# Local attention of a hybrid decoder: the last head pair's projection, two of its three chunks placed behind the scores of two units

## The chip, the cores and the metric

The kernel runs on one core of one Trainium2 chip. Its time is the device time of one execution in microseconds (us). Before the change the median of 3 runs is 2169.54 us (2169.17 to 2170.61). A difference of 0.2%, 4.3 us, is about what a measurement of this kernel can tell from no change.

## What is computed

A two-layer decoder reads 1024 prompt tokens and 8 decode tokens (one new token for each of 8 sequences). Layer 0 is gated linear attention with attention to a memory, layer 1 is sliding-window attention with attention to a memory; each has an MLP. The change lies in the mixer of layer 1. There the normalised tokens are projected to 12 query heads of width 64 and to 4 memory queries. Each query block of 128 tokens looks at the 128 tokens before each of its tokens; 12 query heads share 4 key/value heads, a learned sink joins the softmax, and a bias depends on the distance:

```python
q, qm = split_cols(h @ w_in_b[bl], IN_B_SIZES)
...
def sink_attention(q, k, v, bias, valid, sinks):
    s = jnp.einsum('...qhgd,...khd->...hgqk', q, k).astype(jnp.float32) * (SWA_HEAD_DIM ** -0.5) + bias
    s = jnp.where(valid, s, -jnp.inf)
    sink = sinks.astype(jnp.float32).reshape(SWA_KV_HEADS, SWA_GROUP)[:, :, None, None]
    m = jnp.maximum(jnp.max(s, axis=-1, keepdims=True), sink)
    p = jnp.exp(s - m)
    p = (p / (jnp.sum(p, axis=-1, keepdims=True) + jnp.exp(sink - m))).astype(v.dtype)
    return jnp.einsum('...hgqk,...khd->...qhgd', p, v)
...
mix = jnp.concatenate([o_main, o_mem], axis=-1) @ w_out[l]
```

The 8 decode tokens do the same against cached keys and values (127 positions and their own), and attend to cached memories of 256 positions.

## The kernel before

Activations lie transposed: 128 partitions by 8 slabs of the model width by tokens, in three chunks of 384, 384 and 264 tokens (`CH`; the third holds the last 256 prompt tokens and the 8 decode tokens). Each chunk is kept as a high part and a low part (tiles `xh0`, `xl0` to `xh2`, `xl2`), weights likewise (`wh`, `wl`), and `proj` (L255) multiplies each of the 8 slabs three times: 24 matmuls in one PSUM bank for one block of 128 output features and one chunk.

`in_b(m)` (L1905) is the query projection of head pair m: it loads and splits the pair's weight, then runs `proj` for the three chunks. Each result is scaled into `q` by one DVE operation (L1912), which frees its PSUM bank. The banks come from a pool of two (`mmps`, names `mm`), taken in turn.

`swa(t, i2)` (L1914), called a unit here and written (t, i2), is local attention of head pair t for the two query blocks 2·i2 and 2·i2+1. There are 6 times 4 units. A unit's steps are:

- scores on PE (L1937) into the double bank `sA`, of which there is one; or, for t of 4 and 5 with i2 of 0 and 2, into two banks `mm`;
- four reductions on DVE (L1945), which read the scores, add the bias and take the maximum; then small operations (L1949, L1951);
- four exponentials on ACT (L1959) with sums, two small operations on DVE (L1961, L1963), and one multiplication of the 128 by 768 tile `z` on DVE (L1965);
- six transposes on PE (L1971, L1974) into the double bank `sT`, of which there is one, and its copy to `pt` on ACT (L1976);
- 32 value products on PE (L1982) into banks `sf` and `sx`, and two copies to `q` on ACT (L2005).

`swa_dec()` is local and memory attention of the decode tokens. It is a generator: each of the eight units with t of 4 and 5 first runs its next piece. Its buffers are cut from the tiles of X, which no one needs once the projections are done: `Arena(["xl2", "xh2", "xh1", "xl1", "xh0"])`. Of the eight memory key tiles (`in_mem_kT`, 256 KB each) two fall in `xl2`, four in `xh2` and the last two in `xh1`; the cached keys (`in_swa_kT`) fill the rest of `xh1`, the cached values (`in_swa_v`) and a zeroed query tile lie in `xl1`, and bias and results in `xh0`. All these names print as `ar`. Its loads are issued by POOL, and a load into a tile of X waits for the last matmul that reads that tile. Its steps on the engines are: copies of the memory query (L528, DVE), memory scores (L544, PE, with L554 to L560 on DVE behind), eight copies of the local query (L2036, DVE), local scores (L2050, PE), its softmax (L2054 to L2064), two transposes with four copies (L2068, L564, L2071, L567), and the value products (L2079, and L544 again).

Before the change the loop over t is: for t up to 4 `in_b(t)`, at t of 3 also `in_b(5)` directly behind it, then the four units of t. `in_b(4)` thus stands between the units of t=3 and those of t=4 in the program's text.

The order on each engine is not that of the text. A scheduler goes through the instructions, knows their data dependencies, their buffers and the priorities that the text gives, and writes a fixed order for each engine; engines then work strictly through their lists and wait on semaphores for each other. `add_manual_dep(a, b, NOSYNC)` adds to that planning that a comes behind b on the engine; it adds no wait.

After the last unit the output projection `out_proj` follows: `make_o1` splits `q` into a high and a low part (casts L158 on ACT, L159 on DVE), and 8 feature blocks by 24 matmuls run for each chunk.

## Time and profile before

| | |
|---|---|
| median of 3 runs | 2169.54 us (2169.17 to 2170.61) |
| the profiled execution | 2170.4 us, its span 2168.5 us |
| PE busy | 2130.6 us (98% of the span) |
| DVE, ACT, POOL busy | 1519.3 us (70%), 1092.4 us (50%), 117.1 us (5%) |
| mean granted TensorE clock | 0.997 |

All places below are given in us from the start of the span. PE is TensorE's matmuls, PEld its weight loads, DVE VectorE, ACT ScalarE, POOL GpSimd; a number with L is a line of the kernel. In a row of the timeline stand start, duration, engine, line, operation, output and input tile, shapes and count; a bracket gives the idle time just ahead of it and what ended it. Matmuls overlap, so a row's duration is longer than the step from one matmul to the next. In a row of windows stand the stretch, its length, the busy time of PE, PEld, DVE, ACT and POOL with the number of instructions, the granted TensorE clock (1.00 is full), the DMA engines' share and GB/s. Local attention takes from 1268 to 1417 us; the last eight units begin at about 1367.

### The profile page before, as it was taken

The numbers are of one execution on the slowest core, as the hardware profiler recorded it, in microseconds if no ns is written. First come the engines' busy times: TensorE is split into PE (matmuls) and PEld (weight loads), VectorE is DVE, ScalarE is ACT, GpSimd is POOL, SyncE is SP. The second block draws the span as 40 slices with busy tenths as digits, with TensorE's granted clock in tenths as the row PEclk, the third lists the DMA queues.
The fourth block names the chain that finished last, engine by engine and source line by source line (L and its number), as shares of the span: only waits on it lengthen the run. The fifth ranks groups of instructions, "written<-read, shape, count | busy, mean of one in ns | idle before, by whom it ended". The sixth has DMA issues, their size and how long they took to land.

```text
span 2168.5 us, 41912 instructions
## 1 busy us (share of the span) xinstructions
PE 2130.6 (98%) x16934; PEld 2037.4 (94%) x16934; DVE 1519.3 (70%) x2838; ACT 1092.4 (50%) x2196; POOL 117.1 (5%) x178
## 2 busy tenths in 40 slices
PE   8999999999999999999999999899999999999998
PEld 6879999899999999999999878699999999999998
DVE  7646648768887776856787355647987777764767
ACT  6354536557545444333654354646755545433453
POOL 0012000000000000134100000200000000000011
PEclk9999999999999999999999999999999999999999
DMA  5412026543654459666444201524374345935244
GB/s 170 145 68 76 24 66 171 158 131 126 197 162 129 141 163 324 223 229 233 148 133 151 63 11 32 166 65 157 116 221 142 133 162 208 325 117 172 96 135 148
DMA packets 141670, 316.39 MB, mean 146 GB/s; under 512 B 15833, under 2 KB 57873, under 8 KB 141121
## 3 DMA queue, kind: packets, MB, share of 16 engines
q1 hardware_dynamic: 123552, 268.32, 38.7%
q0 software_dynamic: 8880, 32.54, 4.5%
q10 hardware_dynamic: 9040, 12.82, 1.6%
q8 instruction: 134, 2.20, 0.4%
q14 instruction: 64, 0.52, 0.1%
HBM read 220.97 MB, written 93.74 MB: 145 GB/s over the span
## 4 chain that ended last, share of the span: by engine, by line
PE 89%; DVE 4%; ACT 3%; DMA 3%; issue 1%; SPq 0%; ACTq 0%; DVEq 0%
PE mm L263 17%; PE mx L263 9%; PE mx L851 6%; PE mx L853 6%; PE mx L852 6%; PE mx L1089 5%; PE mx L1090 5%; PE mx L1091 5%; PE mm L851 3%; PE mm L853 3%; PE mm L852 3%; PE mm L1089 2%; PE mm L1090 2%; PE mm L1091 2%; PE sx L1089 1%; PE sx L1091 1%
## 5 line engine op out<-in xcount | busy, mean ns | idle before, releaser
L158 ACT CAST wh<-ws 128x512 fp32r<-128x512 f32 (+1 forms) x258 | 185.8, 722 | 312.4 <-PE mx L852 99.4
L851 PE MATMUL mx<-xf,wh 128*128 128x258 f32 x1048 | 296.9, 283 | 0.0
L853 PE MATMUL mx<-xf,wl 128*128 128x258 f32 x1048 | 295.7, 282 | 0.0
L852 PE MATMUL mx<-xf,wh 128*128 128x258 f32 x1048 | 295.5, 282 | 0.0
L263 PE MATMUL mm<-xh,wh 128*128 128x384 f32 (+1 forms) x864 | 282.0, 326 | 1.5 <-DVE qx L1874 0.6
L263 PE MATMUL mm<-xh,wl 128*128 128x384 f32 (+1 forms) x864 | 278.4, 322 | 0.0
L263 PE MATMUL mm<-xl,wh 128*128 128x384 f32 (+1 forms) x864 | 277.9, 322 | 0.0
L159 DVE TENSOR_TENSOR wl<-ws,wh 128x512 fp32r<-128x512 f32 (+1 forms) x258 | 210.4, 817 | 53.7 <-ACT wh L158 48.0
L158 ACT CAST wh<-wr 128x1024 fp32r<-128x1024 f32 x102 | 106.9, 1048 | 276.8 <-PE sx L1090 261.3
L1089 PE MATMUL mx<-sa,wh 128*128 128x258 f32 x840 | 237.4, 283 | 0.0
L1090 PE MATMUL mx<-sa,wh 128*128 128x258 f32 x840 | 235.9, 281 | 0.0
L1091 PE MATMUL mx<-sa,wl 128*128 128x258 f32 x840 | 235.9, 281 | 0.0
L159 DVE TENSOR_TENSOR wl<-wr,wh 128x1024 fp32r<-128x1024 f32 x102 | 126.5, 1240 | 137.1 <-ACT wh L158 136.9
L852 PEld LDWEIGHTS mx<-xf,wh 128*128 128x128 f32 x1048 | 198.0, 189 | 0.4
L851 PEld LDWEIGHTS mx<-xf,wh 128*128 128x128 f32 x1048 | 197.6, 189 | 0.4
L853 PEld LDWEIGHTS mx<-xf,wl 128*128 128x128 f32 x1048 | 197.8, 189 | 0.0
L263 PEld LDWEIGHTS mm<-xh,wh 128*128 128x128 f32 x864 | 162.7, 188 | 11.2 <-issue 6.3
L263 PEld LDWEIGHTS mm<-xl,wh 128*128 128x128 f32 x864 | 162.7, 188 | 6.8 <-issue 5.3
L263 PEld LDWEIGHTS mm<-xh,wl 128*128 128x128 f32 x864 | 162.4, 188 | 6.9 <-issue 4.9
L1089 PEld LDWEIGHTS mx<-sa,wh 128*128 128x128 f32 x840 | 159.0, 189 | 0.1
L1090 PEld LDWEIGHTS mx<-sa,wh 128*128 128x128 f32 x840 | 158.7, 189 | 0.1
L1091 PEld LDWEIGHTS mx<-sa,wl 128*128 128x128 f32 x840 | 158.3, 188 | 0.0
(578 smaller groups left out, 5783.2 us busy)
## 6 DMA issues: line engine op xcount, KB each, us to landing
ra<-awd SPq DMA_DIRECT2D x92, 516.0 KB, 4.0
ws<-in_w_up SPq DMA_DIRECT2D x64, 512.0 KB, 4.9
wr<-in_w_downb SPq DMA_DIRECT2D x64, 512.0 KB, 5.8
awd<-aw SPq DMA_DIRECT2D x26, 1032.0 KB, 7.7
awd<-am SPq DMA_DIRECT2D x28, 774.0 KB, 8.4
ws<-in_w_in_a SPq DMA_DIRECT2D x20, 512.0 KB, 3.8
ws<-in_w_out SPq DMA_DIRECT2D x16, 512.0 KB, 3.6
ra<-awd SPq DMA_DIRECT2D x28, 258.0 KB, 3.1
```

Source lines behind the costliest of these rows:

```text
L158: nc.scalar.copy(hi, src)
L159: (eng or nc.vector).tensor_tensor(lo, src, f32(hi), ALU.subtract)
L263: mm = nc.tensor.matmul(ps[:M, :n], w_[:, k, :M], x_[:, k, :], start=(i == 0), stop=(i == 3 * KT - 1))
L851: nc.tensor.matmul(ps, wh(k), xh, start=(k == 0), stop=False)
L852: nc.tensor.matmul(ps, wh(k), xl, start=False, stop=False)
L853: mm = nc.tensor.matmul(ps, wl(k), xh, start=False, stop=(k == n - 1))
L1089: nc.tensor.matmul(ps, wh[:, q, ms], h, start=(jj == 0 and q == 0), stop=False)
L1090: nc.tensor.matmul(ps, wh[:, q, ms], lo, start=False, stop=False)
L1091: mm = nc.tensor.matmul(ps, wl[:, q, ms], h, start=False, stop=end)
```

## The change

`in_b(4)` moves up: it now stands behind `in_b(3)`, where `in_b(5)` stood. Behind it follow the load of the weight of head pair 5 and its third chunk alone. The first and second chunk are written behind the units (4, 0) and (4, 1): `proj` gets a name of an instruction, `behind`, and its first matmul is planned behind that one, which is the last score matmul of the unit (`mark`). The number of matmuls, their shapes and the DVE operations behind them stay the same.

```diff
-    def proj(ps, w, hl, n, M=P, fine=False, low_last=False):
+    def proj(ps, w, hl, n, M=P, fine=False, low_last=False, behind=None):
...
             mm = nc.tensor.matmul(ps[:M, :n], w_[:, k, :M], x_[:, k, :], start=(i == 0), stop=(i == 3 * KT - 1))
+            if behind and i == 0:
+                tc.add_manual_dep(mm.ins, behind, NOSYNC, reason="behind a unit")
...
-            def in_b(m):
-                w = wload(wA, wfd[4 + m])
-                for c in range(3):
+            mark = [None]
+
+            def in_b(m, chunks=(0, 1, 2), w=None, behind=None):
+                w = w or wload(wA, wfd[4 + m])
+                for c in chunks:
...
-                    proj(ps, w, hl, n)
+                    proj(ps, w, hl, n, behind=behind)
...
+                mark[0] = row.prev
...
             for t in range(6):
-                if t < 5:
+                if t < 4:
                     in_b(t)
                 if t == 3:
-                    in_b(5)
+                    in_b(4)
+                    w5 = wload(wA, wfd[9])
+                    in_b(5, (2,), w5)
                 if t == 4:
                     dec = swa_dec()
                 for i2 in range(NB // 2):
                     if t >= 4:
                         next(dec, None)
                     swa(t, i2)
+                    if t == 4 and i2 < 2:
+                        in_b(5, (i2,), w5, mark[0])
```

In the changed file the lines below L261 stand 2 to 9 lines lower: the scores are L1941 there, the reductions L1950, the decode tokens' scores L546 and L2055.

The list of PE shows what the scheduler makes of it. The first place is the start of the units of t=3. A projection's matmuls carry the name of their bank: before, `mm_1921` is the third chunk of head pair 5 and `mm_1969` the first of head pair 4; `sA_1924` are the scores of unit (3, 0). Before:

```order
L263 MATMUL mm_1921_16410<-xh_1607_14183,wl_1918_16355 128x264
L1937 MATMUL sA_1924_16439<-kf_14482,q_14472 64x64 x4
L1937 MATMUL sA_1924_16439<-kf_14482,q_14472 64x128 x2
L1937 MATMUL sA_1924_16439<-kf_14482,q_14472 64x192 x4
L263 MATMUL mm_1969_16675<-xh_1574_13799,wh_1967_16671 128x384
L263 MATMUL mm_1969_16675<-xl_1575_13800,wh_1967_16671 128x384
L263 MATMUL mm_1969_16675<-xh_1574_13799,wl_1968_16672 128x384
```

After the change `mm_1925` is the third chunk of head pair 5, `sA_1928`, `sA_1939` and `sA_1950` are the scores of units (3, 0) to (3, 2), `mm_1988` and `mm_1989` those of (4, 0), and `sT_1933` the transposes of (3, 0):

```order
L263 MATMUL mm_1925_16442<-xh_1607_14183,wl_1924_16439 128x264
L1941 MATMUL sA_1928_16471<-kf_14482,q_14472 64x64 x4
L1941 MATMUL sA_1928_16471<-kf_14482,q_14472 64x128 x2
L1941 MATMUL sA_1928_16471<-kf_14482,q_14472 64x192 x4
L1941 MATMUL mm_1988_16751<-kf_14482,q_14472 64x64 x2
L1941 MATMUL mm_1989_16752<-kf_14482,q_14472 64x64 x2
...
L1941 MATMUL sA_1939_16529<-kf_14482,q_14472 64x192 x8
L1941 MATMUL sA_1950_16587<-kf_14482,q_14472 64x192 x5
L1976 MATMUL sT_1933_16500<-ident_85,z_1926_16468 128x128 x4
```

The 72 projection matmuls of head pair 4 no longer stand between the units of t=3; the scores of (4, 0) have come up behind those of (3, 0). The first chunk of head pair 5 (`mm_1998`) takes one of the two banks of (4, 0), and stands behind the value products of (3, 2) (`pt_1956`):

```order
L1987 MATMUL sx_1958_16624<-pt_1956_16621,vtok1_14483 64x64 x2
L263 MATMUL mm_1998_16808<-xh_1574_13799,wh_1923_16438 128x384
L263 MATMUL mm_1998_16808<-xl_1575_13800,wh_1923_16438 128x384
```

The second place, on PE, is the decode tokens' memory scores (L544, after the change L546). Before, all projections end ahead of the scores of (4, 0), and the scores of units up to (5, 0) stand between them and L544; the rows here are the transposes of (4, 1), one score of (5, 1) (`sA_2074`), L544 and what follows, the transposes of (4, 2):

```order
L1971 MATMUL sT_2026_16950<-ident_85,z_2019_16921 128x128 x4
L1974 MATMUL sT_2026_16950<-ident_85,z_2019_16921 128x128 x2
L1937 MATMUL sA_2074_17213<-kf_14482,q_14472 64x192
L544 MATMUL sx_2000_16860<-ar_1974_16755,ar_1972_16753 32x256
...
L1971 MATMUL sT_2040_17018<-ident_85,z_2032_16988 128x128 x4
```

After the change `mm_2029` is the second chunk of head pair 5, `sA_2049` the scores of (4, 3), `sT_2025` the transposes of (4, 1), and `mm_2034` the scores of (4, 2):

```order
L263 MATMUL mm_2029_16953<-xh_1605_14173,wl_1924_16439 128x384
L1941 MATMUL sA_2049_17077<-kf_14482,q_14472 64x192 x2
...
L1976 MATMUL sT_2025_16924<-ident_85,z_2018_16895 128x128 x4
L1979 MATMUL sT_2025_16924<-ident_85,z_2018_16895 128x128 x2
L1941 MATMUL sA_2049_17077<-kf_14482,q_14472 64x192 x6
L546 MATMUL sx_1999_16834<-ar_1972_16703,ar_1970_16701 32x256
...
L2055 MATMUL sf_2012_16866<-ar_1972_16703,ar_1973_16704 32x128 x16
L1941 MATMUL mm_2034_16990<-kf_14482,q_14472 64x192
```

The decode tokens' two score steps now follow the second chunk with little between, and the scores of (4, 2) stand behind both.

On DVE, before, the reductions of (4, 3) (`z_2047`) and (5, 0) (`z_2060`), like those of (4, 2), stand ahead of the decode tokens' softmax, and (5, 1) (`z_2072`) behind it:

```order
L1945 ISA z_2060_17151,sm_2061_17152<-mm_2063_17155,bias_14487,sinks_14474 128x192
...
L554 TENSOR_REDUCE sm_2009_16885<-sx_2000_16860 128x1
...
L2036 COPY ar_1975_16756<-q_14472 64x4x3 x8
...
L567 COPY ar_1972_16753<-sx_2030_16979 128x8x4 x2
L1945 ISA z_2072_17211,sm_2073_17212<-sA_2074_17213,bias_14487,sinks_14474 128x192
```

After the change the multiplication of (4, 1) (`z_2018`) is the last operation of a unit ahead of that softmax, and (4, 2) (`z_2032`) is the first behind it; the scaling of both moved chunks (L1916) lies in between:

```order
L2018 COPY ar_1972_16703<-kf_14482 128x2x8
L1970 TENSOR_TENSOR z_2018_16895<-z_2018_16895,sm_2024_16921 128x768
L159 TENSOR_TENSOR wl_2117_17414<-ws_2115_17411,wh_2116_17413 128x1024
L556 TENSOR_REDUCE sm_2008_16859<-sx_1999_16834 128x1
...
L2041 COPY ar_1973_16704<-q_14472 64x4x3 x8
L1916 SCALAR_TENSOR_TENSOR q_14472<-mm_1998_16808,r_1598_14125 128x384
L1916 SCALAR_TENSOR_TENSOR q_14472<-mm_2029_16953,r_1622_14382 128x384
...
L569 COPY ar_1970_16701<-sx_2030_16979 128x8x4 x2
L1950 ISA z_2032_16988,sm_2033_16989<-mm_2034_16990,bias_14487,sinks_14474 128x192
```

So the reductions of three units, (4, 2), (4, 3) and (5, 0), and the multiplications of two, (4, 2) and (4, 3), have gone from ahead of the decode tokens' softmax to behind it.

The third place is POOL, which issues the decode tokens' loads. Before, `ar_1974` is `xh1`, `ar_1975` is `xl1`, `ar_1972` and `ar_1973` are `xl2` and `xh2`:

```order
L2015 DMA ar_1975_16756<-in_swa_v 127x2048
L534 DMA ar_1974_16755<-in_mem_kT 128x512 x2
L2012 DMA ar_1974_16755<-in_swa_kT 128x16x127
L521 MEMSET ar_1972_16753 128x512
L523 MEMSET ar_1972_16753 128x512
L534 DMA ar_1972_16753<-in_mem_kT 128x512 x2
L534 DMA ar_1973_16754<-in_mem_kT 128x512 x4
```

After the change `ar_1970` and `ar_1971` are `xl2` and `xh2`, `ar_1972` is `xh1`, `ar_1973` is `xl1` and `ar_1974` is `xh0`; `z_1986` belongs to unit (4, 0):

```order
L523 MEMSET ar_1970_16701 128x512
L525 MEMSET ar_1970_16701 128x512
L536 DMA ar_1970_16701<-in_mem_kT 128x512 x2
L536 DMA ar_1971_16702<-in_mem_kT 128x512 x4
L2046 DMA ar_1970_16701<-in_dec_sink 128x1
L1924 MEMSET z_1986_16748 128x2x64
L2044 DMA ar_1974_16705<-in_dec_bias 128x128
L2020 DMA ar_1973_16704<-in_swa_v 127x2048
L536 DMA ar_1972_16703<-in_mem_kT 128x512 x2
L2017 DMA ar_1972_16703<-in_swa_kT 128x16x127
```

The six key tiles that lie in the third chunk's tiles are loaded first now; the cached values, two key tiles and the cached keys, which lie in the second chunk's tiles, come last.

More of the change, by code (lines that the diff above doesn't have):

```diff
@@ L1920, in swa @@
                     nc.gpsimd.memset(z[:, :, 0, :64], 0.0)
-                if t >= 4 and i2 % 2 == 0:
+                if i2 % 2 == 0 and (t >= 4):
                     ps = [mmps(), mmps()]
```

## The prediction

> **What bounds the kernel now.** I read the page first (busy times, slices, chain), then windows of the stretch that the change touches, then the timeline of PE, DVE, ACT and POOL in it.
>
> ```profile
> PE 2130.6 (98%) x16934; PEld 2037.4 (94%) x16934; DVE 1519.3 (70%) x2838; ACT 1092.4 (50%) x2196; POOL 117.1 (5%) x178
> PE 89%; DVE 4%; ACT 3%; DMA 3%; issue 1%; SPq 0%; ACTq 0%; DVEq 0%
> 1343.00:1367.00 24.00, 23.43 (x288) 19.35 (x288) 13.63 (x57) 13.00 (x49) 3.58 (x6) 1.00 0.30 73
> 1368.00:1370.00 2.00, 1.19 (x31) 0.79 (x23) 1.79 (x7) 0.20 (x1) 2.00 (x5) 1.00 1.05 330
> 1370.00:1372.00 2.00, 1.21 (x16) 0.74 (x16) 2.00 (x14) 0.86 (x5) 1.85 (x4) 1.00 1.02 290
> 1372.00:1374.75 2.75, 0.98 (x18) 0.70 (x19) 2.68 (x21) 2.35 (x13) 0.28 (x1) 1.00 1.02 379
> 1374.75:1385.00 10.25, 9.94 (x91) 6.19 (x93) 6.53 (x29) 6.33 (x26) 2.27 (x5) 0.50 0.76 307
> 1394.00:1398.00 4.00, 3.35 (x62) 2.33 (x66) 2.57 (x12) 0.43 (x2) 0.00 (x0) 1.00 0.00 0
> 1398.00:1402.00 4.00, 3.92 (x74) 2.15 (x66) 2.52 (x17) 2.76 (x11) 0.00 (x0) 1.00 0.02 4
> 1402.00:1408.00 6.00, 4.90 (x79) 3.44 (x80) 5.73 (x27) 6.00 (x19) 0.00 (x0) 1.00 0.00 0
> 1417.00:1460.00 43.00, 43.00 (x246) 42.73 (x245) 13.97 (x17) 16.06 (x26) 0.00 (x0) 1.00 0.24 80
> ```
>
> The kernel as a whole is bound by PE. While units run beside projections (1343 to 1367) PE is busy 23.43 of 24 us. Once the projections are used up, PE waits: 3.38 of 6.75 us busy from 1368 to 1374.75, and the granted clock falls to 0.50 for 10.25 us. There DVE is full. From 1402 to 1408 DVE and ACT are full, since the splits for the output projection join in. From 1417 PE is full again, so what this stretch gains or loses reaches the end undiminished. The question is when the output projection's first matmul can start, now at 1406.44, just after the split that follows the last reductions.
>
> **Step 1: the units of t=3 lose their filler.** Up to 1342.7 nothing moves. Then the third chunk of pair 5 comes ahead of the scores of (3, 0).
>
> ```profile
> 1342.33 0.29 PE L263 MATMUL mm<-xh,wl 128*128 128x264 f32 x1
> 1342.45 0.29 PE L263 MATMUL mm<-xh,wh 128*128 128x264 f32 x1
> 1344.09 0.33 PE L263 MATMUL mm<-xh,wl 128*128 128x384 f32 x1
> 1344.26 0.33 PE L263 MATMUL mm<-xh,wh 128*128 128x384 f32 x1
> 1345.12 0.34 DVE L1945 CUSTOM_DVE_ANT_1 z<-sA,bias,sinks 128x128 f32<-128x128 f32 x1
> 1369.38 0.34 DVE L1945 CUSTOM_DVE_ANT_1 z<-mm,bias,sinks 128x128 f32<-128x128 f32 x1
> 1372.09 0.99 DVE L528 COPY ar<-qx 64x4 f32<-64x4 f32 x8
> 1373.27 0.41 DVE L1945 CUSTOM_DVE_ANT_0 z<-mm,bias,sinks 128x192 f32<-128x192 f32 x1
> 1377.07 0.42 DVE L1945 CUSTOM_DVE_ANT_0 z<-sA,bias,sinks 128x192 f32<-128x192 f32 x1
> ```
>
> From start to start a projection matmul takes 0.12 us (264 columns) or 0.17 us (384). The third chunk is 24 x 0.12 = 2.9 us, to about 1345.8. DVE then has the eight copies L528 ahead of its first reduction; they wait for two clears on POOL (0.5 us each), which wait for that chunk: 1345.8 + 1.0 + 1.0 = 1347.8, against 1345.12 now. From there the units run without filler, at the pace of DVE and ACT; the nearest rows are (4, 2) and (4, 3), whose reductions start at 1373.27 and 1377.07, 3.8 us apart, and (4, 0) to (4, 2), 3.9 us for two. I take 3.5 us for each of (3, 0) to (3, 2), since the first units of a stretch run closer: (3, 3) starts at 1358.3, (4, 0) behind it at 1359.7. The first chunk needs a bank of (4, 0) and the value products of (3, 2) ahead of it, so it starts at about 1362.3. The two chunks are 48 x 0.173 = 8.3 us; with two units' transposes (0.7 us each), value products (0.8) and some 1.5 us of waits the second ends at 1374.3, at full clock.
>
> But from 1345.8 to 1362.3 PE has only six score steps, three transpose steps and three value steps, some 9 us in 16.5 us, and at the start some 1.5 us in 5.5 us. The clock fell after 3.38 of 6.75 us, so I expect it to fall here, at about 1353. Half clock until about 1363 lengthens transposes and value products on the path and the head of the first chunk: I take 2 us. Call the end of the second chunk E: 1376.3, with bounds 1371 (pace 2.7 us, no half clock) and 1379.5 (the whole first chunk at half clock, pace 3.8).
>
> The Trainium skill ("TensorE: Matmul & The Clock Gate", Part 1) has the clock halved after an idle window of about 3.4 us and full again after a busy one of that length. This trace differs on both: the clock fell with no wait of PE over 1.44 us in the stretch, and took 10.25 us of nearly full work to return. By the page the first stretch would keep its clock and E would be 1374.3.
>
> ```profile
> 1374.65 0.56 PE L1937 MATMUL mm<-kf,q 64*64 64x64 f32 x4 [1.44 <-DVE sm L1945]
> ```
>
> **Step 2: the decode tokens' loads become the wait.** Cached values, two key tiles and cached keys need `xl1` and `xh1`, so they start at E.
>
> ```profile
> 1360.23 0.34 PE L263 MATMUL mm<-xh,wl 128*128 128x384 f32 x1
> 1360.69 0.56 POOL L2015 DMA_DIRECT2D ar<-in_swa_v  x1 [3.02 <-PE mm L263]
> 1361.24 1.10 POOL L534 DMA_DIRECT2D ar<-in_mem_kT  x2
> 1362.33 1.17 POOL L2012 DMA_DIRECT2D ar<-in_swa_kT  x1
> ar<-in_mem_kT POOLq DMA_DIRECT2D x8, 256.0 KB, 8.1
> ar<-in_swa_v POOLq DMA_DIRECT2D x1, 1016.0 KB, 7.2
> ar<-in_swa_kT POOLq DMA_DIRECT2D x1, 1016.0 KB, 11.9
> ```
>
> Before, the last reader ended at about 1360.5. Values landed at 1360.69 + 7.2 = 1367.9, key tiles by their median at about 1369.5, cached keys at 1362.33 + 11.9 = 1374.2: 7.4, 9.0 and 13.7 us behind the last reader. PE did not feel it, because its list had units until L544 at 1382.01. Now the list has, behind the second chunk, only two parts of scores, value products and one set of transposes, about 2.5 us; then L546 waits for the two key tiles, and DVE, ACT and the rest of PE wait with it. Landing at E + 9.0, bounded by values ahead (7.4) and cached keys behind (13.7); I take 9.0, the rows' own. From there, by the same steps before:
>
> ```profile
> 1382.01 0.65 PE L544 MATMUL sx<-ar,ar 128*32 128x256 f32 x3
> 1385.48 0.42 DVE L554 TENSOR_REDUCE sm<-sx 128x1 f32<-128x256 f32 x1 [2.88 <-PE sx L544]
> 1387.30 0.36 DVE L560 TENSOR_SCALAR ar<-ar,sm 128x256 f32<-128x256 f32 x1
> 1389.25 1.04 DVE L2036 COPY ar<-q 64x12 f32<-64x12 f32 x8
> 1389.79 1.39 PE L2050 MATMUL sf<-ar,ar 128*32 128x128 f32 x32 [0.80 <-issue]
> 1391.25 0.35 DVE L2054 CUSTOM_DVE_ANT_0 ar<-sf,ar,ar 128x128 f32<-128x128 f32 x1 [0.95 <-PE sf L2050]
> 1394.02 0.28 DVE L567 COPY ar<-sx 128x32 f32<-128x32 f32 x2
> 1394.21 0.41 DVE L1945 CUSTOM_DVE_ANT_0 z<-sA,bias,sinks 128x192 f32<-128x192 f32 x1
> ```
>
> Memory scores 3.5 us (1382.01 to 1385.48, at half clock, as here after a wait of 6 us); their softmax 1.5 (2.2 less another unit's multiplication between); copies 1.0; local scores 1.5; softmax, transposes, copies 3.0 (1391.25 to 1394.3); 0.1 between: 10.6 us. So the reductions of (4, 2) start at E + 19.6 = 1395.9. Before, DVE left the same copies at 1394.2. That alone is +1.7 us. The two shifted 1016 KB copies, the clears and the value loads on POOL come behind and are not waited for there; the moved weight split (1.2 us on DVE) hides in the wait.
>
> **Step 3: what is left behind that point.** Before, at 1394.2 the next reductions are those of (5, 1). Now three units' reductions and two multiplications more lie behind it.
>
> ```profile
> L1959 ACT ACTIVATE z<-z,sm 128x192 f32<-128x192 f32 (+1 forms) x48 | 21.0, 442 | 12.4 <-DVE sm L1949 8.6 <-DVE sm L1951 3.8
> L1965 DVE TENSOR_TENSOR z<-z,sm 128x768 f32<-128x768 f32 x12 | 11.5, 956 | 0.2
> L1945 DVE CUSTOM_DVE_ANT_0 z<-sA,bias,sinks 128x192 f32<-128x192 f32 x30 | 11.4, 411 | 4.7 <-PE sA L1937 4.6
> L1976 ACT COPY pt<-sT 128x768 f32<-128x768 f32 x12 | 9.6, 802 | 4.2 <-PE sT L1974 4.2
> 1406.44 0.44 PE L263 MATMUL mm<-xh,wh 128*128 128x384 f32 x1 [0.54 <-ACT xh L158]
> 1407.09 0.41 DVE L1945 CUSTOM_DVE_ANT_0 z<-sA,bias,sinks 128x192 f32<-128x192 f32 x1
> ```
>
> DVE: 12 reductions x 0.34 (start to start) = 4.0, less 0.1; small operations 1.1; two multiplications x 0.9 = 1.8: 6.8 us. ACT: 12 exponentials x 0.44 and their sums, 5.7 us in all, and two copies x 0.7: 7.1 us. Idle time from 1394 to 1408 that can take some of it: DVE 3.2 us, ACT 4.8 us by the windows; most of it is the softmax chain of a unit waiting for itself, and with more units in a row the same waits recur. So the extra is at least 3.6 (6.8 - 3.2) and at most 7.1; I take 5.2. The end of the last reductions, and with it the output projection, moves by 1.7 + 5.2 = +6.9 us. PE's own work does not change: the chunks' 8.3 us are only moved.
>
> The sum: 2170.4 (the profiled execution: span 2168.5 and 1.9 around) + 6.9 = 2177.3; the median lies 0.9 lower, so 2176.4. Bounds: E = 1371 and 7.4 for the landing give 1389.0, -5.2 + 3.6 = -1.6 us (2168); E = 1379.5 and full extra give +4.9 + 7.1 = +12 us (2181.5), with a landing up to E + 13.7 some 4.7 more.
>
> **Rivals.** 0.2%, 4.3 us, is what a measurement can tell from no change.
>
> 1. *The tail absorbs it.* The reductions of three units fill the idle time of DVE and ACT from 1394 to 1402; then the extra is 3.6 at most and E early enough for the rest: 0 to +4.3 us, 2172. For it: ACT has 0.43 us of work from 1394 to 1398. Against: that idle time waits for PE and for DVE.
> 2. *Faster: the chunks fill the hole.* The filler that PE lacks from 1368 to 1385 (3.4 us idle, some 5 us from half clock) is what the two chunks bring. This decides only if the loads don't: with 19.6 us behind E and 5.2 us more, the sum is zero at E = 1369.4, and -4.3 us at E = 1365. Pair 5's first chunk would have to start about 9 us earlier than I find. If it did, some 8 us of idle and half clock would be saved at most; 2163.
> 3. *The clock holds* in the stretch without filler: E = 1374.3, the rest as forecast, +4.9 us, 2174.4. For it: from 1402 to 1408 PE was 82% busy at full clock, so gaps alone don't lower it. Against: 1368 to 1374.75 was no sparser than the start of that stretch will be. The rule of the Trainium skill's page on the clock gate, named above, would have it so.
> 4. *Heavier:* a landing near E + 13.7, or half clock again in the last units: +14 us, 2183.5.
>
> That the scheduler ignores the placing is excluded by the order: the chunks moved. But the first stands behind (3, 2)'s value products, so it fills units of t=3, not the last eight.
>
> **Chances.** Forecast (+4.4 to +12) 0.56; tail absorbs 0.17; faster 0.07; clock holds 0.14, a quarter of it within 0.2%; heavier 0.06. Slower 0.56 + 0.11 + 0.06 = 0.73, same 0.20, faster 0.07. The range 2170.5 to 2183 leaves out the faster case, heavier ones and the low end of the absorbed: about 0.18.
>
> **What would show it.** Right: PE sparse from about 1346 to 1362 with the clock at 0.50 in it; the second chunk's end near 1376; a wait of PE of 5 us or more for DMA just ahead of L546, with DVE and ACT idle; the reductions of (4, 2) near 1396; the output projection's first matmul near 1413; later stages unchanged. Wrong: no DMA wait at L546 (step 2 falls, and 1 or 2 is true); a full clock from 1346 to 1362 (3); reductions of (4, 2) near 1396 but the output projection before 1410 (1).

## The result

| | median, us | runs, us | profiled execution, span, us | mean clock |
|---|---|---|---|---|
| before | 2169.36 | 2168.79 to 2170.61 | 2168.5 | 0.997 |
| after | 2184.4 | 2179.93 to 2184.99 | 2181.3 | 0.993 |

The change makes the kernel slower: the ratio is 1.0064, with a 95% interval of 1.005 to 1.0077, about 14 us. I had forecast slower by 7 us, in a range that ended at 2183.0.

All times below count from one mark that lies just ahead of everything the change moves: the multiplication on DVE that scales the third chunk of pair 2's projection, at 1330.99 us before and 1330.05 us after. Seen from it, the output projection's first matmul comes at 75.5 us before and at 90.3 us after, 14.9 us later. By the first matmul of that projection that goes to an extra bank (`mx`) 13.8 us are left, and from there to the end both executions take the same 751.8 us. So the whole loss lies in this stretch.

The windows of the changed kernel, columns as in the prediction (PE, PEld, DVE, ACT, POOL busy, PE's clock, share of the DMA engines, GB/s):

```profile
1346.00:1350.00 4.00, 1.15 (x24) 0.56 (x16) 2.94 (x20) 1.77 (x9) 3.60 (x7) 1.00 0.86 297
...
1353.40:1356.80 3.40, 3.30 (x42) 2.08 (x44) 1.76 (x12) 1.82 (x6) 0.00 (x0) 0.50 0.00 0
...
1356.80:1360.20 3.40, 3.40 (x22) 2.09 (x21) 1.16 (x3) 2.61 (x12) 0.20 (x1) 0.50 0.02 5
...
1382.00:1386.00 4.00, 0.00 (x0) 0.00 (x0) 0.00 (x0) 0.00 (x0) 1.75 (x4) 0.78 0.98 242
...
1387.65:1391.05 3.40, 3.40 (x32) 1.51 (x32) 0.00 (x0) 0.00 (x0) 0.00 (x0) 0.50 1.09 341
...
1394.60:1404.80 10.20, 8.86 (x92) 5.47 (x89) 6.48 (x42) 3.78 (x18) 1.52 (x4) 0.50 0.56 209
...
1405.00:1417.00 12.00, 10.95 (x165) 8.01 (x163) 10.50 (x42) 9.69 (x40) 0.00 (x0) 1.00 0.01 3
...
1430.00:1470.00 40.00, 40.00 (x229) 39.73 (x228) 10.87 (x13) 14.98 (x25) 0.00 (x0) 1.00 0.26 86
```

The bare units of t=3 start with PE idle for most of 4 us, then run at half clock. From 1382 to 1386 PE, DVE and ACT do nothing at all while the DMA engines are full. Half clock comes three times (to about 1360, to about 1391, and from 1394.6 to 1404.8), 27.3 us in all, where before it came once, for 10.2 us.

The rows of the timeline that mark the steps of the prediction:

```profile
1346.68 0.35 DVE L1950 CUSTOM_DVE_ANT_1 z<-sA,bias,sinks 128x128 f32<-128x128 f32 x1
...
1349.07 0.42 DVE L1950 CUSTOM_DVE_ANT_0 z<-sA,bias,sinks 128x192 f32<-128x192 f32 x1 [0.82 <-PE sA L1941]
...
1355.04 0.42 DVE L1950 CUSTOM_DVE_ANT_0 z<-sA,bias,sinks 128x192 f32<-128x192 f32 x1 [3.02 <-PE sA L1941]
...
1360.53 0.42 DVE L1950 CUSTOM_DVE_ANT_0 z<-sA,bias,sinks 128x192 f32<-128x192 f32 x1 [1.39 <-PE sA L1941]
...
1378.02 0.34 PE L263 MATMUL mm<-xh,wl 128*128 128x384 f32 x1
...
1378.48 0.56 POOL L2020 DMA_DIRECT2D ar<-in_swa_v  x1 [4.86 <-PE mm L263]
...
1387.62 0.65 PE L546 MATMUL sx<-ar,ar 128*32 128x256 f32 x3 [6.26 <-DMA ar<-in_mem_kT]
...
1391.31 0.42 DVE L556 TENSOR_REDUCE sm<-sx 128x1 f32<-128x256 f32 x1 [10.60 <-PE sx L546]
...
1392.83 1.03 DVE L2041 COPY ar<-q 64x12 f32<-64x12 f32 x8
...
1393.89 1.02 DVE L1916 SCALAR_TENSOR_TENSOR q<-mm,r 128x384 f32<-128x384 f32 x2
...
1400.24 0.42 DVE L1950 CUSTOM_DVE_ANT_0 z<-mm,bias,sinks 128x192 f32<-128x192 f32 x1 [1.18 <-PE mm L1941]
...
1420.37 0.42 PE L263 MATMUL mm<-xh,wh 128*128 128x384 f32 x1
```

In order: the first reductions of (3, 0), (3, 1), (3, 2) and (3, 3); the last row of the second late chunk, which ends at 1378.4 (E); the first load, issued at once; the memory scores, after a wait of 6.26 us for a key tile; their softmax; the copies of the decode queries; the multiplications of both late chunks; the reductions of (4, 2); the output projection. One row surprised me: L1916. The first late chunk was complete at about 1373, yet its multiplication ran at 1393.89, behind the decode copies L2041. I had seen that order and had not asked what forced it.

### The profile page after: what moved, and what is told of

Its sections match the earlier page's. It is cut to its first block, busy times and chain, and to the rows that moved or that the text cites. A ratio compares the mean times of both kernels' runs of the same rounds, so it can differ in the third digit from the quotient of the medians.

```text
span 2181.3 us, 41914 instructions
## 1 busy us (share of the span) xinstructions
PE 2136.8 (98%) x16934; PEld 2041.0 (94%) x16934; DVE 1520.8 (70%) x2838; ACT 1092.4 (50%) x2196; POOL 115.9 (5%) x178
## 3 DMA queue, kind: packets, MB, share of 16 engines
q1 hardware_dynamic: 123552, 268.32, 38.4%
## 4 chain that ended last, share of the span: by engine, by line
PE 86%; DVE 6%; issue 3%; ACT 3%; DMA 3%; POOL 0%; SPq 0%; ACTq 0%; DVEq 0%; POOLq 0%
PE mm L263 15%; PE mx L263 8%; PE mx L853 6%; PE mx L855 6%; PE mx L854 6%; PE mx L1091 5%; PE mx L1092 5%; PE mx L1093 5%; PE mm L853 3%; PE mm L855 3%; PE mm L854 3%; PE mm L1091 2%; PE mm L1092 2%; PE mm L1093 2%; PE sx L1091 1%
## 5 line engine op out<-in xcount | busy, mean ns | idle before, releaser
L159 DVE TENSOR_TENSOR wl<-ws,wh 128x512 fp32r<-128x512 f32 (+1 forms) x258 | 210.2, 816 | 51.1 <-ACT wh L158 45.4
```

What stands on the lines that cost most here:

```text
L159: (eng or nc.vector).tensor_tensor(lo, src, f32(hi), ALU.subtract)
```

## The experiments

Single times of one kernel differ by up to 13 us, in part for a reason that lies far from the change (last section), so beside each median stand places in the profiled execution, in us from the mark. "Late end" is the end of the last late chunk (E), "scores" the first memory score (L546), "(4, 2)" its first reduction, "out" the output projection's first matmul, "half" the length of the stretches of half clock that begin between the mark and that projection (of e3's 23.9 us the last 6.0 lie behind it).

| kernel | median, us | ratio to before, 95% | late end | scores | (4, 2) | out | half |
|---|---|---|---|---|---|---|---|
| before | 2169.4 | | none | 51.0 | 42.3 | 75.5 | 10.2 |
| after | 2184.4 | 1.0064 (1.005 to 1.0077) | 48.3 | 57.6 | 70.2 | 90.3 | 27.3 |
| e1 | 2182.8 | 1.0058 (1.0037 to 1.008) | 47.5 | 50.3 | 66.7 | 87.2 | 20.5 |
| e2 | 2178.1 | 1.0033 (1.0022 to 1.0043) | 41.0 | 50.2 | 62.8 | 83.6 | 20.5 |
| e3 | 2183.9 | 1.0058 (1.0036 to 1.008) | 47.2 | 65.5 | 55.9 | 86.6 | 23.9 |
| e4 | 2174.2 | 1.0018 (1.0008 to 1.0028) | 41.1 | 44.3 | 59.0 | 79.7 | 20.5 |
| e5 | 2182.4 | 1.0055 (1.0038 to 1.0072) | 47.2 | 56.5 | 51.1 | 84.6 | 13.6 |
| e6 | 2175.5 | 1.0026 (1.0015 to 1.0037) | 47.4 | 50.3 | 53.8 | 79.4 | 3.4 |
| e7 | 2182.6 | 1.0053 (1.0036 to 1.007) | 45.4 | 54.9 | 67.4 | 87.5 | 17.1 |
| e8 | 2169.1 | 0.9986 (0.9972 to 1.0) | 41.1 | 44.3 | 47.1 | 76.4 | 13.6 |
| e9 | 2170.2 | 0.9998 (0.9989 to 1.0007) | 41.6 | 44.6 | 47.8 | 73.9 | 0.0 |
| e10 | 2177.0 | 1.0025 (1.0014 to 1.0036) | none | 57.1 | 53.2 | 79.0 | 13.6 |
| e11 | 2168.9 | 0.9992 (0.9983 to 1.0001) | 41.6 | 45.8 | 45.6 | 72.4 | 0.0 |
| e12 | 2171.4 | 1.0005 (0.9996 to 1.0015) | 39.6 | 46.2 | 43.5 | 76.4 | 10.2 |

Each place is read from one profiled execution, so a difference of a microsecond or two is not certain: the units of t=3 are the same code in after, e1, e3, e5 and e6, and the first reduction of (3, 3) lies at 29.1 to 30.5 in them. What "out" loses or gains on before agrees with the difference of the medians within 3.2 us (the worst is e10, 3.5 against 6.7). Over whole runs e1, e3, e5 and e7 can't be told from after, since their intervals overlap with its own; what they gain is read from the profile alone.

**e1: the late chunks exchanged.** My theory after the result was the prediction's: the loads hang on E, and the wait is the loss.

```
-                        in_b(5, (i2,), w5, mark[0])
+                        in_b(5, (1 - i2,), w5, mark[0])
```

> The change with its two late chunks exchanged: the second chunk is placed behind the scores of (4, 0), the first behind those of (4, 1). Same work, same places on PE; only the tiles that come free first differ (xh1 and xl1, which the last key tiles, cached keys and cached values wait for, now about 6 us earlier, at about 1372.8 instead of 1378.4). Theory (the decode loads are gated by the end of the chunk that reads xh1 and xl1, and that wait is a term of the loss of its own): the wait of 6.3 us ahead of the decode tokens' memory scores shrinks to under 1 us, these start at about 1382 instead of 1387.6, the end comes 5 to 7 us earlier than with the change: 2178 (2175 to 2181). Rival (the loss sits in the units of t=3 alone, and the decode chain would have taken as long anyway): the second chunk's end stays at 1378 and the time at 2184 (2182 to 2186).

The mechanism came as expected, though 2.0 us of the wait are left instead of under 1, and the gain did not come. Timeline and DMA issues (KB each, median us from issue to landing):

```profile
1381.30 0.42 PE L546 MATMUL sx<-ar,ar 128*32 128x256 f32 x3 [2.01 <-DMA ar<-in_mem_kT]
...
1392.44 0.35 DVE L2059 CUSTOM_DVE_ANT_0 ar<-sf,ar,ar 128x128 f32<-128x128 f32 x1 [5.40 <-DMA ar<-in_dec_bias]
```
```profile
ar<-in_dec_bias POOLq DMA_DIRECT2D x1, 64.0 KB, 13.5
```

The memory scores start 7.3 us earlier from the mark, at full clock. But a load of 64 KB took the place of the wait: the decode bias lies in `xh0`, which now comes free last, and behind some 4.5 MB of other loads and copies it took 13.5 us to land (2.2 us after the change alone). DVE waits 5.4 us for it. Only 3.1 us reach the output projection. The wait for loads is a term, but taking away one load shows the next.

**e2: pair 4 behind the units of t=3 again.**

```
-                if t < 4:
+                if t < 5:
                     in_b(t)
                 if t == 3:
-                    in_b(4)
                     w5 = wload(wA, wfd[9])
```

> The change with pair 4's projection back where it was before, behind the units of t=3; pair 5's last chunk early and its first two behind the scores of (4, 0) and (4, 1) as in the change. The units of t=3 have filler again. Theory (lost filler and half clock in the units of t=3 make E late, and the loads hang on E): no half clock from 1351 to 1361; units of t=3 at 3 to 4 us each; E, the end of the second late chunk, at about 1374 instead of 1378.4; the wait for the loads behind it stays, about 6 us; time 2180 (2176 to 2183). Rival 1 (the clock costs nothing there): E within 1 us of 1378, time 2184. Rival 2 (the lost filler is nearly all of the loss, the loads would be hidden): time within 4 us of before, 2169 to 2173.

As the theory said, and stronger: E is 7.3 us earlier, the wait behind it is the same, and the output projection comes 6.7 us earlier.

```profile
1383.98 0.65 PE L546 MATMUL sx<-ar,ar 128*32 128x256 f32 x3 [6.23 <-DMA ar<-in_mem_kT]
```

**e3: decode steps later.** It was meant to show that the order of the lists makes the wait cost.

```
-                    if t >= 4:
+                    if t >= 4 and (t, i2) not in ((4, 1), (4, 2)):
                         next(dec, None)
```

> The change with the decode tokens' steps behind their loads taken up two units later, so that the memory scores stand behind the scores of (4, 2), (4, 3) and (5, 0) in PE's order, as before; the loads are issued as in the change. Theory (the wait for the loads costs because the in-order lists put the decode steps ahead of three units): E unchanged at 1378; the reductions of (4, 2) at about 1381 instead of 1400; no wait of 5 us with PE, DVE and ACT all idle; 9 to 15 us earlier than the change, 2171 (2168 to 2177). Rival (the landing itself sets the end: the decode chain behind it is as long as what is left of the units): 2180 to 2185.

This theory fell. The scores of (4, 2) did move ahead of the memory scores in PE's list, and yet its reductions came at 55.9, not at the expected 51, and the output projection only 3.7 us earlier:

```profile
1385.46 1.19 DVE L2041 COPY ar<-q 64x12 f32<-64x12 f32 x8 [2.83 <-POOL ar L2033]
...
1386.69 1.02 DVE L1916 SCALAR_TENSOR_TENSOR q<-mm,r 128x384 f32<-128x384 f32 x2
...
1387.30 1.65 PE L1941 MATMUL mm<-kf,q 64*64 64x192 f32 x16 [2.79 <-DVE q L1916]
...
1410.59 0.42 DVE L574 COPY ar<-sx 128x256 f32<-128x256 f32 x1 [4.59 <-PE sx L546]
```

Read upward, this is a chain: the scores of (4, 2) wait for the multiplications that empty the late chunks' banks; these stand behind the decode copies; the copies wait for the clear of their target on POOL (L2033, in `xl1`); the clear waits for E and stands behind seven DMA issues. Later, the memory values, which reuse the key tiles' places, come late in turn (DVE waits 4.59 us for their products).

**e4: only the first chunk late**, with everything else as before, behind the scores of (4, 1).

```
                 if t == 3:
+                    w5 = wload(wA, wfd[9])
+                    in_b(5, (1, 2), w5)
...
+                    if t == 4 and i2 == 1:
+                        in_b(5, (0,), w5, mark[0])
```

> The order of before (pair 4 behind the units of t=3) with one difference: only the first chunk of pair 5 is placed late, behind the scores of (4, 1); the second and third come early. So xh1 and xl1 come free as before, and 4.2 us of projection move into the stretch in which PE waited and fell to half clock. Theory (the change loses by the gated loads and by the bare units of t=3, not by a chunk behind the scores as such): no wait for loads, (4, 0) about 4 us earlier than before, less or no half clock behind it; 2164 (2160 to 2168), faster than before. Rival (a chunk behind the scores costs by itself, by delaying the reductions behind it on PE): 2170 to 2176.

The rival held: 4.2 us later at the output projection, with no bare unit and no wait for key tiles. (DVE waits 4.23 us for the two small decode loads that now issue last.) (4, 2) moved from 42.3 to 59.0. One late chunk is enough to throw the decode tokens' softmax ahead of three units.

**e5: the copies split.** From e3 and e4 I formed a new theory. The copies L2041 read the decode columns of three pairs at once, so the stretch of memory from a copy's first to its last element covers pair 5's first two chunks as well, which the late multiplications write. Before, all of pair 5 was written ahead of them.

```
-                            nc.vector.tensor_copy(qmk[rows, pr, e::2, c : c + 5 : 2],
-                                                  q[rows, 3 * pr : 3 * pr + 3, SEQ + e : NT : 2].rearrange("p t g -> p g t"))
+                            for a, b in ((0, 3),) if pr == 0 else ((0, 2), (2, 3)):
+                                nc.vector.tensor_copy(qmk[rows, pr, e::2, c + 2 * a : c + 2 * b - 1 : 2],
+                                                      q[rows, 3 * pr + a : 3 * pr + b, SEQ + e : NT : 2].rearrange("p t g -> p g t"))
```

> The change with the decode tokens' copies out of the queries of pairs 3 to 5 written as two copies each (pairs 3 and 4, then pair 5), so that the stretch of memory from a copy's first to its last element no longer covers pair 5's first two chunks. Same values, four copies more (12 instead of 8). The late chunks' multiplications no longer stand behind these copies in DVE's order, and the scores of (4, 2), (4, 3) and (5, 0) now stand ahead of the decode tokens' softmax. Theory (the multiplications of the late chunks were ordered behind the decode copies, these behind the clear on POOL and the loads, and (4, 2) needs the banks that the multiplications free; this order, not the load itself, is the largest term): E unchanged at 1378, memory scores still about 9 us behind it, but reductions of (4, 2) at about 1382 to 1384 instead of 1400; output projection's first matmul 9 to 13 us earlier than with the change; 2173 (2168 to 2177). Rival (the load and the half clock set the end all the same): 2180 to 2185.

The order changed as expected for (4, 2) and (4, 3); the reductions of (5, 0) still stand behind the memory scores' softmax. In DVE's list the multiplication of the second late chunk now comes straight behind the weight split, ahead of (4, 2), and the copies stand some fifty rows further down:

```profile
1383.83 0.54 DVE L1916 SCALAR_TENSOR_TENSOR q<-mm,r 128x384 f32<-128x384 f32 x1
...
1385.42 0.42 DVE L1950 CUSTOM_DVE_ANT_0 z<-mm,bias,sinks 128x192 f32<-128x192 f32 x1 [1.05 <-PE mm L1941]
...
1394.14 0.42 DVE L556 TENSOR_REDUCE sm<-sx 128x1 f32<-128x256 f32 x1 [4.46 <-PE sx L546]
```

(4, 2) comes 19 us earlier from the mark. But of these only 5.7 reach the output projection, half of what I expected: the memory scores still wait for the load at E + 9.3, and behind their softmax (4.46 us of DVE's wait) stand (5, 0) and all that follows. The time, 2182.4, lies in the rival's range, and the order is not shown to be the largest term: pair 4's place (e2) brought 6.7 us.

**e6: split copies, and no load behind the last chunk.** The chunks are exchanged as in e1, and the decode bias goes at the stage's start into the tile that the kernel calls `spare`.

```
-        vp.tile([P, 128], F32, tag="spare", name="spare")
+        dbias = vp.tile([P, 128], F32, tag="spare", name="spare")
...
+            nc.sync.dma_start(dbias, A["dec_bias"])
...
-                dbias = ap.tile([P, P], F32, tag="dbias", name="dbias", bufs=1)
-                nc.gpsimd.dma_start(dbias, A["dec_bias"])
```

> As the split copies, and the two late chunks exchanged, and the decode bias (64 KB) loaded at the stage's start into a tile of its own, so that no load of the decode tokens waits for the last chunk. Theory (what is left of the loss after the split is the wait for loads at E + 9 and its half clock): no wait of PE or DVE for DMA over 1.5 us between 1378 and 1400; 2 to 6 us less than with the split alone: 2169 (2165 to 2173). Rival (with units ahead of the decode softmax the loads are covered already): within 1 us of the split alone.

Another 5.2 us, as the theory said; the one wait for DMA that is left is 1.72 us of PE, just over the 1.5 expected, and half clock is down to 3.4 us. (The time, 2175.5, lies above the range because e5's already did.) The order alone brings 5.7 us (e5), the order and the loads together 10.9. What the loads bring alone is not measured: in e1 (3.1 us) the bias still waits for the last chunk.

**e7: more work at the start of t=3.** Eight matmuls that nobody uses behind the scores of each of (3, 0) to (3, 2), 2.9 us of PE at full clock.

```
+                    if t == 3 and i2 < 3:
+                        ps = mmps()
+                        for k in range(8):
+                            mm = nc.tensor.matmul(ps[:, :264], w5[0][:, k, :], X[0][0][0][:, k, :264],
+                                                  start=(k == 0), stop=(k == 7))
+                            if k == 0:
+                                tc.add_manual_dep(mm.ins, mark[0], NOSYNC, reason="behind a unit")
```

> The change with eight extra projection matmuls (264 columns, 0.12 us each at full clock) behind the scores of each of (3, 0), (3, 1) and (3, 2), written to a bank that nobody reads: 2.9 us of PE work more, nothing less. Theory (half clock, from the sparse PE at the start of t=3, makes E late): the clock stays at 1.00 in most of 1347 to 1361, (3, 3)'s reductions come 2 to 4 us earlier and E lies 1 to 3 us earlier although there is more to do; time 2 us less than the change, 2182 (2180 to 2184). Rival (the pace there is that of DVE and ACT, or the clock falls anyway): E 0 to 3 us later, 2185 to 2188.

```profile
1350.00:1366.00 16.00, 13.17 (x192) 9.61 (x183) 11.87 (x63) 8.91 (x36) 4.48 (x10) 1.00 0.38 131
...
1353.77 0.42 DVE L1950 CUSTOM_DVE_ANT_0 z<-sA,bias,sinks 128x192 f32<-128x192 f32 x1 [0.82 <-PE sA L1941]
...
1358.11 0.42 DVE L1950 CUSTOM_DVE_ANT_0 z<-sA,bias,sinks 128x192 f32<-128x192 f32 x1 [1.39 <-PE sA L1941]
...
1362.42 0.42 DVE L1950 CUSTOM_DVE_ANT_0 z<-sA,bias,sinks 128x192 f32<-128x192 f32 x1
```

The rows are the first reductions of (3, 1), (3, 2) and (3, 3). The clock held through the bare units, E came 2.9 us earlier and the output projection 2.8 us, with more to do and nothing left out. That is the price of half clock there, less what the added work costs; against the other kernels with the same units (e1, e3, e5, e6, with E at 47.2 to 47.5) it is 1.8 to 2.1 us. Of the 6.7 us that real filler brought in e2, this leaves 3.9 that a held clock alone did not bring.

**e8: e4 with split copies and the early bias.**

> The order of before with only pair 5's first chunk placed late, behind the scores of (4, 1), plus the split copies and the early decode bias. Theory (the chunk placed behind the scores costs nothing by itself; what cost was the order of the multiplications behind the decode copies): without the copies' order, 4.2 us of projection fill the stretch in which PE waited: faster than before, 2165 (2161 to 2169). Rival (the chunk delays the units behind it by its own length): 2170 to 2175.

The split and the early bias together take 3.3 us off e4 at the output projection. But the chunk gained nothing over before: 76.4 against 75.5 in the stretch, and a median 1.4 us lower than that of before in the same comparison, with an interval that reaches 1.0. The theory's 4 us are not there: half clock still comes twice, 3.4 us at the chunk itself and 10.2 us behind it.

**e9: all three causes taken away**, e6 with pair 4 back behind the units of t=3 (e2's edit).

> All three causes taken away at once, with two chunks of pair 5 still placed behind the scores of (4, 0) and (4, 1): pair 4's projection back behind the units of t=3, the late chunks exchanged and the decode bias loaded early, and the copies of the decode queries split. Theory (the loss of 14.9 us at the output projection's first matmul is the sum of separate terms: 5.7 for the order behind the copies, 5.2 for loads behind the last chunk, 6.7 for the bare units of t=3, and late chunks as such cost nothing): 14.9 - 17.6 = -2.7, time 2168 (2165 to 2171), a little faster than before. Rival (the terms overlap: an earlier E was worth 6.7 us only because the loads hung on it): 2171 to 2175.

```profile
1336.00:1366.00 30.00, 29.26 (x393) 23.43 (x397) 17.38 (x76) 16.52 (x63) 4.66 (x10) 1.00 0.13 40
...
1378.00:1398.00 20.00, 13.21 (x201) 8.40 (x199) 12.53 (x66) 9.83 (x38) 4.66 (x9) 1.00 0.88 313
```

16.5 of 17.6 us came back: 73.9, which is 1.6 us ahead of before, with no half clock anywhere in the stretch. So the three terms nearly add. No run gives the order of before the split copies and the early bias alone, so it is not shown that two late chunks cost nothing: they may cost what these two edits bring. Over all runs the time is that of before.

**e10: the change without the placing**, pair 4 and all of pair 5 ahead of the units of t=3.

```
-                    in_b(5, (2,), w5)
+                    in_b(5, (0, 1, 2), w5)
...
-                    if t == 4 and i2 < 2:
-                        in_b(5, (i2,), w5, mark[0])
```

> The change without the placing: pair 4, then all three chunks of pair 5 ahead of the units of t=3; no chunk behind any unit. All twelve units of t=3 to 5 then run without filler, but no load and no copy hangs on a late chunk. Theory (bare units of t=3 are a term of their own, of some 4 us, paid with the clock): half clock for most of t=3, (4, 0) only 1 to 2 us later than before, time 2173 (2170 to 2177), well below the change. Rival 1 (nothing but the placing of the chunks behind the units costs): 2170 or less. Rival 2 (bare units cost most): 2180 or more.

3.5 us later at the output projection than before, with 13.6 us at half clock; (4, 0) comes 2.5 us later (40.9 against 38.4), a little more than expected, and the clock is at half for 6.8 of the 15 us of t=3, not for most of them. The time stands at the edge of the theory's range: twelve bare units cost 3.5 us in the stretch and 3.0 to 7.8 us over whole runs, not 14.

**e11 and e12: later decode steps, once the copies are out of the way** (the first unit's delay of e3's edit, on e9 and on e8).

> The kernel with all three causes taken away (pair 4 behind the units of t=3, late chunks exchanged, decode bias early, split copies), and the decode tokens' steps behind their loads taken up one unit later. The scores of (4, 2) now stand ahead of the memory scores on PE. Theory (with the copies no longer in the way, later decode steps put units into the wait for key tiles): the 1.6 us wait of PE ahead of the memory scores goes, reductions of (4, 2) 3 to 5 us earlier (at 43 to 45 us from the anchor instead of 47.8), the output projection's first matmul 1 to 3 us earlier; time 2168 (2166 to 2170.5). Rival (the decode steps' own chain sets the end, and comes later now): 2171 to 2175.

> Only pair 5's first chunk placed late, behind the scores of (4, 1), with split copies and early decode bias, and the decode steps behind their loads one unit later. Theory: scores of (4, 2) and (4, 3) ahead of the memory scores; reductions of (4, 2) 3 to 5 us earlier than without the delay (48.2 us from the anchor); output projection's first matmul 1 to 3 us earlier (76.4); time 2167.5 (2165 to 2170). Rival (the decode chain sets the end): 2169 to 2173.

e11 is the earliest of all at the output projection, 72.4, 3.1 us ahead of before; later decode steps, which brought little in e3, bring 1.5 us over e9 here, in one execution each. Its median is 2168.9, against 2170.6 for before in the same comparison; the ratio is 0.9992 with an interval that reaches 1.0001, so over whole runs it can't be told from before. e12 moved (4, 2) 3.6 us and the output projection not at all, as its rival said; that the decode chain sets the end there is argued, not shown.

## Why the prediction was right in direction and short by half

The direction, the places and the chain held. PE is sparse from 1346 with half clock behind it; PE, DVE and ACT idle ahead of L546, 6.26 us, for a key tile; the landing is E + 9.3 us (forecast 9.0); later stages are unchanged. Four sizes, counted on the scale of before (0.94 us added to the rows above), make the error of 8.0 us at the output projection (+6.9 forecast, +14.9 measured). The steps that failed are the first three, each a term of the sum that was too small:

- **Step 1, E: 1379.3 against 1376.3, 3.0 us.** The first reduction was right (1347.6 against 1347.8). From there to (3, 3) I had 10.5 us, 3.5 a unit, and 2 us in all for half clock. The three units took 2.4, 6.0 and 5.5 us, 13.9 in all; at full clock (e7, with its added work) they took 2.4, 4.3 and 4.3, 11.0 in all, and the last of them 4.2 in e6. So half clock cost 2.8 us, 0.8 more than I took, and the pace at full clock was 0.5 us over mine. The rest came at full clock behind it: from (3, 3) to the first late chunk 4.6 us against 4.0, and from that chunk's start to E 13.2 against 12.0.
- **Step 2, memory scores to (4, 2): 12.6 us against 10.6.** I added the steps up as rows of before, and behind the memory scores those ran at full clock. Here the clock was at 0.50 again from 1394.5. Local scores still ran at full clock and took what they took before (1.40 and 1.39 us); the value products behind them took 1.8 us against 1.1, and the last twelve score matmuls of (4, 2) 1.54 us, where fourteen of that form took 0.87 before. That is 1.5 of the 2.0 us.
- **Step 3, (4, 2) to the output projection: 20.1 us against 17.4.** The extra was 7.9 us, more than the 7.1 that I called its upper bound. Half clock covers the first 4.5 us of this part. No run with this order has this part without half clock; where it covers 7.0 (e1), 7.4 (e4) and 7.5 us (e2), the part is 20.5, 20.7 and 20.8 us long. Drawn on to no half clock at all, these give some 19 us, an estimate. By it about 1 us of the 2.7 is half clock, and the rest stays open.
- **The landing:** 0.3 us.

The rows for steps 1 and 2 are, from e6, the first reductions of (3, 2) and (3, 3) at full clock; from after, the local scores and the last scores of (4, 2); and from before, score matmuls of the same form at full clock:

```profile
1359.77 0.42 DVE L1951 CUSTOM_DVE_ANT_0 z<-sA,bias,sinks 128x192 f32<-128x192 f32 x1 [2.89 <-PE sA L1942]
...
1364.01 0.42 DVE L1951 CUSTOM_DVE_ANT_0 z<-sA,bias,sinks 128x192 f32<-128x192 f32 x1 [0.35 <-PE sA L1942]
```
```profile
1393.36 1.40 PE L2055 MATMUL sf<-ar,ar 128*32 128x128 f32 x32 [2.11 <-DVE ar L2041]
...
1398.67 1.54 PE L1941 MATMUL mm<-kf,q 64*64 64x192 f32 x12
```
```profile
1388.11 0.87 PE L1937 MATMUL mm<-kf,q 64*64 64x192 f32 x14
```

So the mechanism was right and three terms were too small. Half clock beyond what I had counted makes about 3.3 of the 8.0 us (0.8, 1.5 and the estimated 1); the larger part was lost at full clock, most of it between (3, 3) and E and behind (4, 2). I had let half clock come in the units of t=3 and, in the price of the memory scores, behind the wait; it came a third time, from 1394.5. This is the rival that I called "heavier" (half clock again in the last units, 2183.5) and gave 6 in 100. The evidence against that chance stood in my own sum: behind the memory scores it has 2.5 us of softmax and copies in which PE has little to do, and the clock had fallen before after PE was busy for 3.38 of 6.75 us.

"The clock holds" was excluded by the first window of half clock; "the tail absorbs it" by 7.9 us extra; "faster" by E. But that rival was not empty: in e9 and e11, with the three causes gone, the clock stays full through the stretch and the output projection comes 1.6 and 3.1 us earlier than before in one execution each, though over whole runs neither can be told from before.

The explanation of the order was incomplete, and no number of the forecast shows it. I took it as given that the decode softmax stands ahead of three units. e5 shows that for two of them, (4, 2) and (4, 3), this follows from the copies and the multiplications sharing a stretch of `q`. That the scheduler compares first and last elements is my reading; what is shown is that splitting the copies at pair 5 undoes the order.

## What to carry to other kernels

Before placing work later, list what its result and its operands hold up: the bank that it fills, the buffers that it reads, and every later instruction whose address range spans its output, though it reads none of it; and look in the order for the consumer that now stands behind a stranger. Price a stretch that loses its filler at both clocks (here 4.2 to 4.3 us a unit at full clock, 5.5 to 6.0 with half clock), and look for every later wait of PE that can bring half clock back. Taking away one wait can bring out the next (in e1 the 6.3 us for a key tile became 2.0, and 5.4 for the bias), so an experiment that removes one says little until the other is gone too.

## What the runs showed of the hardware

**Half clock comes in pieces of 3.4 us.** The time at half clock in the stretch is 3.4, 10.2, 13.6, 17.1, 20.5, 23.9 or 27.3 us in these kernels, all multiples of 3.4. After the change the three falls were followed by about 10.2, 6.8 and 10.2 us. The stretches of 3.4 us just ahead of a fall:

```profile
1371.35:1374.75 3.40, 1.33 (x27) 0.70 (x19) 3.33 (x25) 3.00 (x16) 0.77 (x2) 1.00 1.01 361
```
```profile
1346.60:1350.00 3.40, 0.88 (x16) 0.56 (x16) 2.37 (x15) 1.77 (x9) 3.00 (x6) 1.00 0.89 300
...
1380.85:1384.25 3.40, 0.51 (x12) 0.14 (x2) 0.00 (x0) 0.60 (x1) 2.90 (x6) 1.00 1.04 239
...
1391.10:1394.50 3.40, 1.23 (x36) 0.78 (x32) 2.45 (x13) 0.56 (x2) 2.93 (x6) 1.00 1.33 501
```

The first is of before, the others of after: PE was busy for 0.51 to 1.33 us of 3.40, so none of them was idle throughout. The busy time sets no clear threshold: the clock fell at 1407.22 in e5 after 2.03 us of 3.41, and held in e12 (six such stretches ahead of its fall at 1389.20) after 1.66:

```profile
1403.81:1407.22 3.41, 2.03 (x51) 1.48 (x44) 2.60 (x12) 1.57 (x5) 0.00 (x0) 1.00 0.41 151
```
```profile
1365.31:1368.73 3.42, 1.66 (x9) 1.69 (x10) 3.38 (x23) 1.01 (x6) 3.07 (x7) 1.00 0.94 283
```

A window of about 3.4 us is what the Trainium skill states ("TensorE: Matmul & The Clock Gate", Part 1), and these traces agree with its length. They do not agree that an idle window is needed for the fall, and one busy window did not always end it: 3.40 of 3.40 us busy from 1387.65 brought the clock back, while 3.41 of 3.41 from 1394.51 left it at half for two such stretches more.

```profile
1394.51:1397.92 3.41, 3.41 (x45) 2.03 (x38) 1.44 (x7) 1.11 (x5) 0.33 (x1) 0.50 0.46 167
```

**A fall far upstream is part of the scatter.** In eight of these fourteen profiled executions, code that no kernel changes ran between 100 and 110 us at a mean clock of 0.51 to 0.85, in the others at 1.00:

```profile
100.00:110.00 10.00, 9.32 (x59) 6.71 (x59) 4.97 (x6) 4.95 (x14) 0.00 (x0) 1.00 0.01 2
```
```profile
100.00:110.00 10.00, 10.00 (x31) 5.99 (x32) 3.03 (x4) 3.52 (x10) 0.00 (x0) 0.51 0.01 2
```

The first is of after, whose mark lies at 1330.05, the second of e10, whose mark lies at 1337.03. The marks of the eight lie at 1333.2 to 1337.0, those of the other six at 1330.1 to 1333.1. What decides the fall is open, and it is not the whole scatter: e3 had none there, and its mark lies 3.1 us behind that of after. These shifts are as large as the effects that e8 to e12 were to tell apart, which is why they are read in the stretch.
